# A chunked recurrence woven into projections: the order of its narrow matmuls and of three short VectorE and ScalarE steps

## The chip, the cores and the metric

The kernel runs on one core of one Trainium2 chip. The metric is the device time of one execution in microseconds. Before the change it is 2709.11 us, the median of 3 runs (2707.46 to 2709.36). A difference is read in per cent of that.

The engines are PE (TensorE: matmuls; PEld is its weight load), DVE (VectorE), ACT (ScalarE), POOL (GpSimd) and SP, which issues the DMAs. Each of them runs its own instructions in the order in which they were built, and they wait for one another by semaphores.

## The reference

One encoder layer over 2048 tokens of width 1024. A combined input projection `h @ w_in` feeds two branches: a bidirectional gated linear recurrence (HGRN2) of 8 heads of width 128, and neighbourhood attention of 16 heads of width 64. Both are gated, concatenated, projected out and normalised. The change is in the recurrence. Cut to that:

```python
b = jnp.cumsum(log_f, axis=3)
scores = jnp.einsum('bhntd,bhnsd->bhnts', q * jnp.exp(b - b_mid), k * jnp.exp(b_mid - b))
scores = jnp.where(lower_tri, scores, 0.0)
o_intra = jnp.einsum('bhnts,bhnsv->bhntv', scores, v)
def step(state, xs):
    qc, kc, vc, dc = xs
    o = jnp.einsum('bhtd,bhdv->bhtv', qc, state)
    state = dc[..., None] * state + jnp.einsum('bhtd,bhtv->bhdv', kc, vc)
    return state, o
...
o = direction(zf_fw, lb_fw, False) + direction(zf_bw, lb_bw, True)
o = _rmsnorm(o.transpose(0, 2, 1, 3), norm_g).reshape(B, S, HG_WIDTH)
return o.astype(g_in.dtype) * jax.nn.silu(g_in)
```

The two directions are computed with chunked scores inside a chunk and a state that passes between chunks. The output of each head is divided by the root of the mean of its squares and gated.

## The kernel before

The work is in float32. Large products are split in a high and a low part (`wh`, `wl`, `h`) and use three matmuls of 512 columns per 128 rows of weights. The program has a start and a first attention half, then the recurrence (16 rounds: 8 heads of the first 1024 tokens, 8 of the second), then the second attention half and the output projection.

**The recurrence.** `hgrn` handles one head of one half: two groups g = 0, 1 of 512 tokens, four chunks of 128 each. For a group:

- `rates` and `ends` make the decay sums `c` (the scans, L422), the factors `ei`, `qi`, `de` and the decays `dec`.
- `turned` (L447 on PE, L449 on ACT) transposes, `updates` (L455) multiplies keys by values per chunk, `forward_states` (L466, L468, DVE) runs the forward state through the four chunks, reading the `updates` result in PSUM.
- `diagonal_factors` (L479 to L485) makes `kx` and `qx`, each with one buffer: differences (L479, DVE), two exponentials (L481, L482, ACT), products (L483, L485, DVE).
- `diagonal` (L494) makes the scores of 32 by 32 blocks with matmuls on a quarter of PE's columns, four of them side by side (`tile_position=(0, j * 32)`).
- `level_factors` (L507 to L515) and `level` (L522) do the same for distances of 32 and 64, with matmuls on half of PE's columns. The factors have four buffers `x`.
- `masked` copies the levels' scores to `pm` (L528, ACT), copies the diagonal's scores by mask to `pdb` (L532, DVE, three per group) and adds them to `pm` (L535, DVE, four per group).
- `outputs` multiplies the values by `pm` (L546) and the forward states by `qi` (L548).

`hgrn_tail` finishes a head while the next one is under way: the backward states (L614, L616) and their products (L620), and in the second half `rms_out`: squares (L320, ACT), split in `rh` (L322, DVE) and `rl` (L324, DVE), summed over the head by two matmuls with ones (L327, L328), then root, product and gate (L330 to L334) and the DMA to `yT`. In the second half it also corrects the first half's tokens (L643, L644) and norms them.

**The order of the work.** PE's order is written by hand (`manual_schedule`). `weave` alternates the recurrence, which yields a number of units (54 per head), with `hgrn_dense`, the projections of the next head (L255, evacuated by ACT at L352 to L369, with L314 to L316 and L372 for the gate). A unit is about 1.5 steps of 3 matmuls, and the dense generator runs until its share is reached. So the number behind a `yield` sets how many projection matmuls stand at that place. `next(tail)` takes one step of the last head's tail. The order on DVE and ACT is set when the program is built: a scheduler takes what it holds for ready, the lowest place in the source first; `tc.high_priority(offset=PRI)` moves an instruction up by 1500 places. Weights come by DMA and are split by L245 (ACT) and L246 (DVE).

In before, the heart of a group reads:

```python
pb = diagonal(kx, qx)
lf = [(w, *level_factors(w, g, cs, ks)) for w in (32, 64)]
yield 6
next(tail, None)
pa = ps("pa")
for w, xk, xq in lf:
    level(w, pa, xk, xq)
pm = masked(pa, pb)
yield 5
outputs(g, v, pm)
```

Of the kernel before, what the change touches and what calls it, by code (L numbers as in the profile page):

```python
# [11 lines left out]
F32R = mybir.dt.float32r  # L12
U32 = mybir.dt.uint32
AF = mybir.ActivationFunctionType
ALU = mybir.AluOpType
# [4 lines left out]
P = 128  # L20
# [10 lines left out]
PRI = 1500  # L31
# [6 lines left out]
def body(ctx: ExitStack, tc: tile.TileContext, t):  # L38
    nc = tc.nc
    dve, act, pool, pe = nc.vector, nc.scalar, nc.gpsimd, nc.tensor  # L40
# [46 lines left out]
    def nm(s):  # L87
        cnt[0] += 1
        return f"{s}_{cnt[0]}"

    def tl(tag, dt=F32, shape=None):
        if tag in cur["smap"]:
            tag = cur["smap"][tag]
            return sh.tile([P, 512], dt, tag=tag, name=nm(tag), bufs=SH[tag])
        return cur["pool"].tile([P, 512] if shape is None else shape, dt, tag=tag, name=nm(tag), bufs=cur["bufs"].get(tag, 1))
# [4 lines left out]
    def ps(tag="mx"):  # L100
        if tag == "pj":
            return pp.tile([P, 512], F32, tag=tag, name=nm("pj"))
        tag = cur["map"].get(tag, tag)
        return cur["psum"].tile([P, 512], F32, tag=tag, name=nm("ps"), bufs=cur["ps"][tag])
# [211 lines left out]
        act.activation(e, e, AF.Exp, scale=-1.0)  # L316

    def rms_out(u, g, o_sb, sg, tok):
        sq = tl("t")
        act.activation(sq, o_sb, AF.Square)  # L320
        sh_ = tl("rh", F32R)
        dve.tensor_copy(sh_, sq)  # L322
        sl_ = tl("rl", F32R)
        dve.tensor_tensor(sl_, sq, sh_, op=ALU.subtract)  # L324
        yield
        pss = ps("ss")
        pe.matmul(pss, ones, sh_, start=True, stop=False)  # L327
        pe.matmul(pss, ones, sl_, start=False, stop=True)  # L328
        r = tl("t")
        act.activation(r, pss, AF.Ln, scale=1.0 / 128.0, bias=eps_rms)  # L330
        act.activation(r, r, AF.Exp, scale=-0.5)
        dve.tensor_mul(r, r, o_sb)
        yv = tl("t")
        dve.tensor_tensor(yv, r, sg, op=ALU.mult)  # L334
        dma(yT[u][:, tok:tok + 512], yv)
# [60 lines left out]
    def hgrn(u, half, st, tail):  # L396

        zs, qs, sgs, vts = st["e"], st["q"], st["sg"], st["v"]
        S = {}
        if half == 1:  # L400
            S[0, 0] = sfb[u]
        ubs, decs, qibs, os_ = {}, {}, {}, {}
        decb_all = tl("decb", shape=[P, 8])

        def rates(d, g):
            col = d * 8 + u
            e = zs[d, g]
            dve.tensor_scalar_min(e, e, ECAP)
            L = tl("g")
            act.activation(L, e, AF.Ln, bias=1.0)  # L410
            c = tl("c")
            act.activation(c, e, AF.Ln, scale=lbt[:, col:col + 1], bias=1.0)
            r = tl("g")
            act.activation(r, L, AF.Exp, scale=-1.0, bias=l1m[:, col:col + 1])
            dve.tensor_tensor(e, e, r, op=ALU.mult)
            for b in range(4):
                lo, hi = b * P, (b + 1) * P
                if d == 0:
                    sl = slice(lo, hi)
                else:  # L420
                    sl = slice(hi - 1, lo - 1 if lo else None, -1)
                dve.tensor_tensor_scan(c[:, sl], c[:, sl], L[:, sl], 0.0, op0=ALU.add, op1=ALU.subtract)  # L422
            return c, e

        def ends(d, g, c, k):
            last = 127 if d == 0 else 0
            ei = tl("ei")
            act.activation(ei, c, AF.Exp)
            dec = tl("dec", shape=[P, 4])
            dve.tensor_copy(dec, v4(ei, P)[:, :, last])  # L430
            decs[d, g] = dec
            if d == 1:
                dve.tensor_copy(decb_all[:, g * 4:g * 4 + 4], v4(ei, P)[:, :, last])
            qi = tl(f"qi{d}")
            dve.tensor_mul(qi, qs[g], ei)
            qibs[d, g] = qi
            de = tl("de")
            for b in range(4):
                sl = slice(b * P, (b + 1) * P)
                act.activation(de[:, sl], c[:, sl], AF.Exp, scale=-1.0, bias=c[:, b * P + last:b * P + last + 1])  # L440
            dve.tensor_mul(de, k, de)  # L441
            return de

        def turned(src, tag):
            pk = ps("tr")
            for b in range(4):
                pe.transpose(pk[:, b * P:(b + 1) * P], src[:, b * P:(b + 1) * P], ident)  # L447
            ke = tl(tag)
            act.activation(ke, pk, AF.Copy)  # L449
            return ke  # L450
# [7 lines left out]
        def forward_states(g, pu):  # L458
            for b in range(4):
                bb = g * 4 + b  # L460
                if half == 0 and bb == 7:
                    sn = sfb[u]
                else:
                    sn = tl("Sf", shape=[P, P])
                if (0, bb) in S:
                    dve.scalar_tensor_tensor(sn, S[0, bb], decs[0, g][:, b:b + 1], pu[:, b * P:(b + 1) * P], op0=ALU.mult, op1=ALU.add)  # L466
                else:
                    dve.tensor_copy(sn, pu[:, b * P:(b + 1) * P])  # L468
                S[0, bb + 1] = sn

        def diagonal_factors(g, cs, ks):
# [16 lines left out]
        def diagonal(kx, qx):  # L488
            pb = ps("pb")
            for b in range(4):  # L490
                for k0, n, dst in ((0, 64, b * 64), (32, 32, 256 + b * 32)):
                    for j in range(4):
                        o = (b * 4 + j) * 64
                        pe.matmul(pb[j * 32:(j + 1) * 32, dst:dst + n], kx[:, o + k0:o + k0 + 32], qx[:, o:o + n],  # L494
                                  start=True, stop=True, skip_group_check=True, tile_position=(0, j * 32))
            return pb

        def level_factors(w, g, cs, ks):
            n2 = 512 // (2 * w)
            xq, xk = tl("x"), tl("x")  # L500
            cv = {d: cs[d].rearrange("p (n s c) -> p n s c", s=2, c=w) for d in range(2)}
            kv = {d: ks[d].rearrange("p (n s c) -> p n s c", s=2, c=w) for d in range(2)}
            xqv = xq.rearrange("p (n s c) -> p n s c", s=2, c=w)
            xkv = xk.rearrange("p (n s c) -> p n s c", s=2, c=w)
            rf = cv[0][:, :, 0, w - 1:w].to_broadcast([P, n2, w])
            rb = cv[1][:, :, 1, 0:1].to_broadcast([P, n2, w])
            dve.tensor_tensor(xkv[:, :, 0, :], rf, cv[0][:, :, 0, :], op=ALU.subtract)  # L507
            dve.tensor_tensor(xqv[:, :, 1, :], cv[0][:, :, 1, :], rf, op=ALU.subtract)
            dve.tensor_tensor(xkv[:, :, 1, :], rb, cv[1][:, :, 1, :], op=ALU.subtract)
            dve.tensor_tensor(xqv[:, :, 0, :], cv[1][:, :, 0, :], rb, op=ALU.subtract)  # L510
            act.activation(xk, xk, AF.Exp)
            act.activation(xq, xq, AF.Exp)
            dve.tensor_mul(xkv[:, :, 0, :], xkv[:, :, 0, :], kv[0][:, :, 0, :])
            dve.tensor_mul(xkv[:, :, 1, :], xkv[:, :, 1, :], kv[1][:, :, 1, :])
            dve.tensor_mul(xq, xq, qs[g])  # L515
            return xk, xq
# [34 lines left out]
        for g in range(2):  # L551
            v = turned(vts[g], "v")
            next(tail, None)
            cs, ks = {}, {}
            cs[0], ks[0] = rates(0, g)
            yield 5
            next(tail, None)
            cs[1], ks[1] = rates(1, g)
            de0 = ends(0, g, cs[0], ks[0])
            yield 5  # L560
            next(tail, None)
            ke0 = turned(de0, "ke")
            de1 = ends(1, g, cs[1], ks[1])
            kx, qx = diagonal_factors(g, cs, ks)
            yield 3
            next(tail, None)
            forward_states(g, updates(ke0, v))
            ke1 = turned(de1, "ke")
            yield 3
            next(tail, None)  # L570
            pu = updates(ke1, v)
            if g == 0:
                ub = tl("ub")
                act.activation(ub, pu, AF.Copy)
                ubs[g] = ub
            else:
                ubs[g] = pu
            pb = diagonal(kx, qx)
            lf = [(w, *level_factors(w, g, cs, ks)) for w in (32, 64)]
            yield 6  # L580
            next(tail, None)
            pa = ps("pa")
            for w, xk, xq in lf:
                level(w, pa, xk, xq)
            pm = masked(pa, pb)
            yield 5
            outputs(g, v, pm)
        for _ in tail:
            pass
# [667 lines left out]
    with psum_phase("h", *HPS), phase("h", HB, SMH), tc.manual_schedule(engines={mybir.EngineType.PE}):  # L1257
        hgrn_init()
        tail = iter(())
        for i in range(16):  # L1260
            half, u = divmod(i, 8)
            if i < 15:
                nxt = hgrn_dense((i + 1) % 8, (i + 1) // 8, i in (6, 7), reload if i == 6 else None)
                tail, st = weave(hgrn(u, half, st, tail), nxt, HTOT, HSUM)
# [235 lines left out]
```

## Time and profile before

| what | value |
|---|---|
| median of 3 runs | 2709.11 us (2707.46 to 2709.36) |
| the profiled execution's own time | 2713.41 us |
| its span | 2711.6 us |
| PE busy | 2613.3 us, 96% of the span |
| DVE busy | 1763.9 us, 65% |
| ACT busy | 1420.5 us, 52% |
| DMA, mean | 109 GB/s |

The span is the time from the first to the last instruction of the profiled execution. A row of the timeline reads: start in us, duration in us, engine, line, operation, names of what is written and read, shape, count, and in brackets the idle time of the engine before it with what ended it. Rows of matmuls give a modelled end, so distances between starts are used for them; a float32 matmul of 128 or 64 columns shows as two records.

### The profile page before, as it was taken

How to read it: one execution, taken by the hardware profiler on the slowest of the kernel's cores; microseconds unless marked ns; L12 is line 12 of the kernel's file. 1: busy time of each engine (PE TensorE's matmuls, PEld its weight loads, DVE VectorE, ACT ScalarE, POOL GpSimd, SP SyncE). 2: the span in 40 equal slices, each digit the busy share in tenths (PEclk: the TensorE clock that was granted, in tenths of full speed). 3: DMA queues.
4: the chain of work that ended last, by engine and by line, in shares of the span. 5: the costliest groups of instructions: out<-in, count | busy, mean ns of one | idle time of the engine just before them, and what ended most of it. 6: DMA issues, size and time to landing. Idle time of an engine off the chain costs nothing.

```text
span 2711.6 us, 46035 instructions
## 1 busy us (share of the span) xinstructions
PE 2613.3 (96%) x17328; PEld 2157.5 (80%) x17328; DVE 1763.9 (65%) x4351; ACT 1420.5 (52%) x2808; POOL 104.9 (4%) x142
## 2 busy tenths in 40 slices
PE   4999999989999999999999999989999999899998
PEld 3788888878888888888888888877777777678887
DVE  5435445467777778877777877455777777648443
ACT  4434344366666666666666666444666666431110
POOL 0000000000000000000000000000000000032221
PEclk9999999999999999999999999999999999999999
DMA  7564454312111126212221222354444444444331
GB/s 248 159 183 139 130 172 139 117 52 75 63 57 61 63 74 218 82 41 75 75 79 59 67 67 86 107 159 119 125 129 126 127 131 138 110 136 140 97 93 55
DMA packets 226845, 296.46 MB, mean 109 GB/s; under 512 B 28743, under 2 KB 117575, under 8 KB 226503
## 3 DMA queue, kind: packets, MB, share of 16 engines
q1 hardware_dynamic: 226623, 293.52, 35.5%
q8 instruction: 136, 2.23, 0.4%
q14 instruction: 86, 0.70, 0.1%
HBM read 218.24 MB, written 66.99 MB: 105 GB/s over the span
## 4 chain that ended last, share of the span: by engine, by line
PE 71%; DVE 3%; DMA 3%; ACT 2%; issue 1%; SPq 0%; DVEq 0%; ACTq 0%
PE pj L255 38%; PE ps L1333 4%; PE ps L1332 4%; PE ps L1331 4%; PE ps L1041 3%; PE ps L1022 3%; PE pj L268 2%; PE ps L455 2%; PE ps L978 1%; PE ps L447 1%; PE ps L981 1%; PE ps L522 1%; PE ps L546 1%; PE ps L494 1%; PE ps L548 1%; DMA bias<-tint 1%
## 5 line engine op out<-in xcount | busy, mean ns | idle before, releaser
L255 PE MATMUL pj<-h,wh 128*128 128x512 f32 x4016 | 1289.2, 402 | 6.5 <-ACT wh L781 2.1
L255 PEld LDWEIGHTS pj<-h,wh 128*128 128x128 f32 x4016 | 728.3, 189 | 168.1 <-issue 21.5
L255 PE MATMUL pj<-h,wl 128*128 128x512 f32 x2008 | 789.1, 393 | 0.1
L255 PEld LDWEIGHTS pj<-h,wl 128*128 128x128 f32 x2008 | 378.6, 189 | 83.7 <-DVE wl L756 0.5
L995 ACT ACTIVATE pbuf<-pbuf,mx 128x480 f32<-128x480 f32 (+2 forms) x256 | 164.3, 643 | 177.5 <-DVE mx L990 176.8
L990 DVE CUSTOM_DVE_ANT_1 pbuf<-ps,bias 128x480 f32<-128x480 f32 (+2 forms) x256 | 144.0, 596 | 139.3 <-PE ps L981 124.7
L268 PE MATMUL pj<-wh,h 128*128 128x256 f32 x1024 | 197.0, 289 | 4.5 <-ACT vt L274 4.2
L268 PEld LDWEIGHTS pj<-wh,h 128*128 128x128 f32 x1024 | 164.5, 194 | 8.5 <-ACT vt L274 5.0
L245 ACT ACTIVATE wh<-wr 128x512 fp32r<-128x512 f32 x192 | 120.1, 626 | 82.4 <-PE pj L255 69.6
L246 DVE TENSOR_TENSOR wl<-wr,wh 128x512 fp32r<-128x512 f32 x192 | 131.7, 686 | 46.8 <-ACT wh L245 46.0
L268 PE MATMUL pj<-wl,h 128*128 128x256 f32 x512 | 146.0, 285 | 0.0
L1028 ACT ACTIVATE pt<-ps 128x512 f32<-128x512 f32 (+1 forms) x128 | 69.0, 539 | 124.6 <-PE ps L1022 124.3
L1026 DVE COPY pt<-ps 128x512 f32<-128x512 f32 (+1 forms) x128 | 79.4, 620 | 78.8 <-PE ps L1022 77.9
L1041 PE MATMUL ps<-pt,V 128*64 128x128 f32 x1408 | 108.3, 285 | 14.9 <-DVE pt L1026 6.0
L441 DVE TENSOR_TENSOR de<-e,de 128x512 f32<-128x512 f32 x64 | 44.3, 692 | 118.3 <-ACT de L440 117.2
L1022 PE MATMUL ps<-ident,pbuf 128*128 128x128 f32 x896 | 119.1, 273 | 0.8 <-DVE pbuf L1000 0.8
L1022 PEld LDWEIGHTS ps<-ident,pbuf 128*128 128x128 f32 x896 | 105.6, 141 | 17.1 <-issue 1.9
L1000 DVE TENSOR_SCALAR pbuf<-pbuf,mx 128x480 f32<-128x480 f32 (+2 forms) x256 | 108.0, 437 | 4.9
L1041 PEld LDWEIGHTS ps<-pt,V 128*64 128x64 f32 x1408 | 75.8, 137 | 43.5 <-issue 19.6
L1307 ACT ACTIVATE yh<-yr 128x512 fp32r<-128x512 f32 x52 | 32.7, 629 | 131.2 <-PE ps L1332 112.8
L268 PEld LDWEIGHTS pj<-wl,h 128*128 128x128 f32 x512 | 99.5, 194 | 0.7 <-issue 0.5
L1380 DVE TENSOR_TENSOR vt<-ps,gt 128x512 f32<-128x512 f32 x24 | 16.5, 692 | 127.2 <-PE ps L1333 127.2
(266 smaller groups left out, 4622.9 us busy)
## 6 DMA issues: line engine op xcount, KB each, us to landing
wr<-in_w_in SPq DMA_DIRECT2D x276, 256.0 KB
V<-nv SPq DMA_DIRECT2D x256, 64.0 KB
yr<-yq SPq DMA_DIRECT2D x64, 256.0 KB
bias<-tint SPq DMA_DIRECT2D x24, 480.0 KB
wr<-in_w_v SPq DMA_DIRECT2D x32, 256.0 KB
x<-in_x SPq DMA_DIRECT2D x32, 256.0 KB
ada<-in_ada_w SPq DMA_DIRECT2D x16, 512.0 KB
nv<-vt SPq DMA_DIRECT2D x32, 256.0 KB
```

What stands on the lines that cost most here:

```text
L245: act.activation(hi, raw, AF.Copy)
L246: dve.tensor_tensor(lo, raw, hi, op=ALU.subtract)
L255: pe.matmul(pz, a, b, start=(k == 0 and n == 0), stop=(k == KT - 1 and n == 2))
L268: pe.matmul(pzs[tp][:, i * 256:(i + 1) * 256], a, b, start=(k == 0 and n == 0 and i == 0), stop=(k == KT - 1 and n == 2), skip_group_check ...
L990: return dve.tensor_tensor_reduce(s[:, 0:nk].rearrange("p (r c) -> p r c", c=32), sc[:, 0:nk].rearrange("p (r c) -> p r c", c=32), bt[:, 0 ...
L995: act.activation(s[:, 0:nk], s[:, 0:nk], AF.Exp, scale=-1.0, bias=mx[:, 0:1], accum_out=mx[:, 1:2])
L1000: dve.tensor_scalar(s[:, 0:nk], s[:, 0:nk], mx[:, 2:3], 1.0, op0=ALU.mult, op1=ALU.mult)
L1022: pe.transpose(ptp[:, c * P:(c + 1) * P], s[:, c * P:(c + 1) * P], ident)
L1041: pe.matmul(self.po[R][hs_, j * P:(j + 1) * P], self.st.V[c0 + c][:, j * P + hh * 64:j * P + hh * 64 + 64], pts[hh][:, c * P:(c + 1) * P], ...
L1331: pe.matmul(pz, yh[:, kk], wh, start=first, stop=False)
L1332: pe.matmul(pz, yh[:, kk], wl, start=False, stop=False)
L1333: pe.matmul(pz, yl[:, kk], wh, start=False, stop=last)
```

## The change

There are three edits, all in the recurrence. The squares and their two parts in `rms_out` are put under `high_priority`. The forward states are put under `high_priority`. And in `hgrn` the call of `diagonal` moves behind the `yield` and the tail's step, directly in front of the levels; the level factors are then traced before it, and the two yields become 5 and 6 where they were 6 and 5.

```diff
     def rms_out(u, g, o_sb, sg, tok):
-        sq = tl("t")
-        act.activation(sq, o_sb, AF.Square)
-        sh_ = tl("rh", F32R)
-        dve.tensor_copy(sh_, sq)
-        sl_ = tl("rl", F32R)
-        dve.tensor_tensor(sl_, sq, sh_, op=ALU.subtract)
+        with tc.high_priority(offset=PRI):
+            sq = tl("t")
+            act.activation(sq, o_sb, AF.Square)
+            sh_ = tl("rh", F32R)
+            dve.tensor_copy(sh_, sq)
+            sl_ = tl("rl", F32R)
+            dve.tensor_tensor(sl_, sq, sh_, op=ALU.subtract)
         yield
...
-                if (0, bb) in S:
-                    dve.scalar_tensor_tensor(sn, S[0, bb], decs[0, g][:, b:b + 1], pu[:, b * P:(b + 1) * P], op0=ALU.mult, op1=ALU.add)
-                else:
-                    dve.tensor_copy(sn, pu[:, b * P:(b + 1) * P])
+                with tc.high_priority(offset=PRI):
+                    if (0, bb) in S:
+                        dve.scalar_tensor_tensor(sn, S[0, bb], decs[0, g][:, b:b + 1], pu[:, b * P:(b + 1) * P], op0=ALU.mult, op1=ALU.add)
+                    else:
+                        dve.tensor_copy(sn, pu[:, b * P:(b + 1) * P])
...
-            pb = diagonal(kx, qx)
             lf = [(w, *level_factors(w, g, cs, ks)) for w in (32, 64)]
-            yield 6
+            yield 5
             next(tail, None)
+            pb = diagonal(kx, qx)
             pa = ps("pa")
             for w, xk, xq in lf:
                 level(w, pa, xk, xq)
             pm = masked(pa, pb)
-            yield 5
+            yield 6
             outputs(g, v, pm)
```

More of the change, by code (lines that the diff above doesn't have):

```diff
@@ L577, in hgrn @@
                 ubs[g] = pu
+            lf = [(w, *level_factors(w, g, cs, ks)) for w in (32, 64)]
+            yield 5
+            next(tail, None)
             pb = diagonal(kx, qx)
-            lf = [(w, *level_factors(w, g, cs, ks)) for w in (32, 64)]
-            yield 6
-            next(tail, None)
             pa = ps("pa")
```

## The prediction

> **What bounds the kernel now.** I read the page's totals first, then the busy time of four stretches, then the list of who waited for whom on PE.
>
> ```profile
> span 2711.6 us, 46035 instructions
> PE 2613.3 (96%) x17328; PEld 2157.5 (80%) x17328; DVE 1763.9 (65%) x4351; ACT 1420.5 (52%) x2808; POOL 104.9 (4%) x142
> ...
> 602.00:900.00 298.00, 298.00 (x2236) 252.62 (x2236) 220.60 (x580) 185.39 (x342) 0.40 (x4) 1.00 0.19 62
> ...
> PE ps L455 <- DVE Sf L466: 8.2, 1, 8.2
> PE ps L327 <- DVE rh L322: 5.6, 9, 1.4
> PE ps L328 <- DVE rl L324: 1.8, 8, 0.2
> PE ps L546 <- DVE pm L535: 0.2, 1, 0.2
> ```
>
> The recurrence lies at about 600 to 1745 us, and there PE is busy all the time (298.00 of 298.00 us) at a granted clock of 1.00, while DVE is busy for 74% (220.60/298.00). Every PE instruction counts there, and so does every wait that PE gets. The change can remove little waiting: the waits on the norm squares (L327, L328) are 7.4 us, the one on the forward states (L455) 8.2 us, and the masked scores (L546) are waited for once, 0.2 us.
>
> **The diagonal moved in front of the levels.** The chain that ended last shows what the narrow matmuls cost around them (start, us, what).
>
> ```profile
> 698.81 0.89 PE ps L455 x8
> 699.71 0.83 PE ps L494 x64
> 700.54 6.33 PE pj L255 x27
> 706.87 1.08 PE ps L522 x32
> 707.95 5.00 PE pj L255 x21
> ...
> 715.17 5.47 PE pj L255 x24
> ```
>
> After the transposes, 24 projection matmuls take 5.47 us, 0.228 each. By that price the 27 after the diagonal (L494) would take 6.15, and take 0.18 more; the 21 after the levels (L522) would take 4.79, and take 0.21 more. So leaving narrow tiles costs some 0.2 us. After the change L494 stands directly before L522, and one of the two exits per group goes, but the step from 32 columns to 64 is in no row. Its bounds are the nearest rows: free (0.18 saved), or as dear as an exit (nothing saved). A loss I exclude within 0.02 us, since no exit is above 0.21. I take the middle, 0.10, for 32 groups (16 heads, two groups each): **-3.2 us**, bounds -5.8 to +0.6.
>
> The Trainium skill, "TensorEngine Tiling (Array Packing)", Key Properties, states that a change of tiling mode, not merely of the tile, drains TensorE. By that rule 32 to 64 columns is a switch too and may cost as much as an exit; the saving would be 0 and my sum 3.2 us higher. The rows agree that leaving a narrow mode costs time, and no row shows this switch.
>
> **What the move does to DVE.** The built order of the two kernels (line numbers of before throughout) shows it; for the groups g = 1:
>
> ```
> before: 532 479 616 479 532 532 616 483 485 485 314 | 507..510 507..510 | 535x4 372
> after:  616 616 314 532 479 479 532 532 | 507..510 507..510 | 372 535x4 483 485 485
> ```
>
> In before, the diagonal's three masked copies (L532) and the next group's differences (L479) ran in the 6.3 us between diagonal and levels. Now they can only begin when the diagonal ends, which is when the levels begin, and they stand ahead of L535, which finishes pm, for which PE waits at L546.
>
> ```profile
> 666.28 0.31 DVE L532 COPY_PREDICATED pdb<-mskd,ps 128x128 f32<-128x128 uint32 x1 [0.71 <-PE ps L494]
> 666.49 1.29 DVE L479 TENSOR_TENSOR kx<-c 128x512 f32<-128x512 f32 x2
> 667.69 0.49 DVE L532 COPY_PREDICATED pdb<-mskd,ps 128x128 f32<-128x128 uint32 x2
> ...
> 1276.59 1.15 PE L522 MATMUL ps<-x,x 128*64 128x64 f32 x32
> ...
> 1277.23 0.43 DVE L314 TENSOR_SCALAR gt<-gt 128x512 f32<-128x512 f32 x1 [1.23 <-ACT gt L369]
> 1277.57 0.42 DVE L507 TENSOR_TENSOR x<-c 128x256 f32<-128x256 f32 x1
> ...
> 1280.26 1.16 DVE L535 TENSOR_TENSOR pm<-pdb 32x128 f32<-32x128 f32 x4
> 1281.45 0.69 DVE L372 TENSOR_TENSOR sg<-gt,gt 128x512 f32<-128x512 f32 x1
> ...
> 1282.58 0.38 PE L546 MATMUL ps<-pm,v 128*128 128x128 f32 x2
> ```
>
> Count from the start of the levels. In before pm was ready at 4.83 (1281.42) and wanted at 5.99. In after it is wanted at 5.99 + 3 x 0.228 = 6.67, because 24 projection matmuls stand there in place of 21. DVE first does L314, which waits for the gate projection's exit on ScalarE; that projection's end lies 24 matmuls behind L455 in both kernels, directly before the diagonal now, so I leave L314 near where it was (0.55; row: 0.64). Then: L314 0.34, copies and differences 1.90 (666.28 to 668.18), eight differences 2.69 (1277.57 to 1280.26), L372 0.61 (its 0.69 less the 0.08 by which these rows overlap), L535 1.16. The end is 0.55 + 6.70 = 7.25, and PE starts some 0.05 later. **PE waits 0.6 us** per group (bounds 0.3 to 1.0). The order is the same in heads 0 to 5 and 8 to 14 (counted 0 to 15 over both halves): 13 x 0.6 = **+7.8 us**. The last head's g = 0, with 18 matmuls in that gap in both kernels, loses about **+1.3 us**: wanted at 1.08 + 5.00 - 3 x 0.228, or nearer 5.5, ready at about 7.0 by the sum below, less the 0.2 us that it waits already.
>
> Groups g = 0 are not caught by this: with 27 matmuls there, pm is wanted 0.68 later, at 7.4. In heads 9 to 14 DVE must first do L644 and L408 (first L532 at about 0.3), then 1.90 + 0.34 (L322) + 2.69 + 0.60 (L324) + 1.16 = 7.0. The cover left is 0.4 us; if it is gone, each of the 15 groups pays what is missing.
>
> **Norm squares and forward states "ahead".** In the built order every L466 and L468 keeps its neighbours, so the forward states gain nothing and the 8.2 us stay: I count 0. The norm squares move in heads 9 to 14, and the wrong way where it counts. First the step after the three products of L620:
>
> ```profile
> 1290.27 0.83 PE L620 MATMUL ps<-qi,Sb 128*128 128x128 f32 x6
> ...
> 1290.47 0.60 ACT L352 ACTIVATE e<-pj 128x512 f32<-128x512 f32 x1 [0.59 <-PE pj L255]
> 1291.13 0.60 ACT L622 ACTIVATE t<-ps 128x512 f32<-128x512 f32 x1
> ...
> 1292.30 0.62 ACT L428 ACTIVATE ei<-c 128x512 f32<-128x512 f32 x1
> 1292.82 0.62 ACT L410 ACTIVATE g<-e 128x512 f32<-128x512 f32 x1
> 1293.35 0.70 ACT L412 ACTIVATE c<-e,lbt 128x512 f32<-128x512 f32 x1
> ...
> 1293.07 0.69 DVE L324 TENSOR_TENSOR rl<-t,rh 128x512 fp32r<-128x512 f32 x1
> 1294.08 1.37 DVE L422 TENSOR_TENSOR_SCAN c<-c,g 128x128 f32<-128x128 f32 x4 [0.32 <-ACT c L412]
> ...
> 1295.75 0.40 PE L327 MATMUL ps<-rh,ones 128*128 128x512 f32 x1
> ```
>
> After's ScalarE order is 352, 428, 622, 315, 410, 412, 320; DVE's is the four scans L422, then 322, 372, 324. From the start of L620: L352 at 0.20, then five steps of 0.50 to 0.55 bring L412 to 2.8, its end to 3.5; scans 1.28, L322 0.34, L372 0.61, L324 0.69: rl is ready at 6.45, where before it was at 3.49. PE wants it at 5.7 (0.23 behind L327's 5.48). **PE waits 0.8 us** x 6 = **+4.8 us** (bounds 0 to 1.2 each).
>
> Second, the norm of the first half's tokens after L643, in the same heads:
>
> ```profile
> 1311.79 1.22 DVE L483 TENSOR_TENSOR qx<-qx,q 128x1024 f32<-128x1024 f32 x1
> ...
> 1319.47 1.16 DVE L535 TENSOR_TENSOR pm<-pdb 32x128 f32<-32x128 f32 x4
> ...
> 1322.40 0.38 PE L546 MATMUL ps<-pm,v 128*128 128x128 f32 x2
> ...
> 1332.04 0.69 DVE L644 TENSOR_TENSOR cl<-ps,cl 128x512 f32<-128x512 f32 x1
> 1333.43 0.43 DVE L322 CAST rh<-t 128x512 fp32r<-128x512 f32 x1 [0.70 <-ACT t L320]
> ...
> 1335.52 0.40 PE L327 MATMUL ps<-rh,ones 128*128 128x512 f32 x1
> 1335.75 0.40 PE L328 MATMUL ps<-rl,ones 128*128 128x512 f32 x1
> ...
> 1305.63 0.49 PE L327 MATMUL ps<-rh,ones 128*128 128x512 f32 x1 [0.37 <-DVE rh L322]
> 1306.36 0.50 PE L328 MATMUL ps<-rl,ones 128*128 128x512 f32 x1 [0.23 <-DVE rl L324]
> ```
>
> Count from L546. Before, L535 ended 1.77 us ahead of it and L644 ended at 10.33: 12.1 us of queue. After, L535 ends about 0.4 ahead, and the queue behind it gains L483 (1.22) and two L485 (of the shape of L479's pair, 1.2; all stood ahead of L535) and loses L324 (0.6) and the pauses in it. Those I take as 0.8 (with none of them gone it is 13.9, with the whole growth covered 12.1): 12.1 + 2.4 - 0.6 - 0.8 = 13.1 us. L644 ends at 12.7, L320 and L322 add 1.13, rh is ready at 13.8. PE wants it at 13.12: **0.7 us**. Where L327 waits for rh, L328 waits for rl too: 0.73 apart at 1305.63 against 0.23 at 1335.52, **0.5 us** more. 6 x 1.2 = **+7.2 us** (bounds 0 to 1.9 each). The waits that stand there already (1305.63) keep their order and follow L328 by the same chain; I count 0 for them. No DMA is added, and the SP queue moves by a few places of weight loads, which I cost at nothing: the weight halves L246 are needed a projection (16 steps) after they are made.
>
> **Sum.** -3.2 + 7.8 + 1.3 + 4.8 + 7.2 = +17.9. Against the profiled execution (2713.41 us, span 2711.6) that is 2731.3; it lies 4.3 above the median of the three runs, 2709.1, so I forecast **2727.0 us**.
>
> **The rivals.**
> - Heavier: the cover of 0.4 us in the g = 0 groups is gone as well (15 heads x 0.6 = 9 more) or each wait is at its upper bound: 2736 to 2746. For it speaks that DVE is busy for 74% on average and does these chains without a pause; against it that it still waits for others at 666.28 (0.71) and 1277.23 (1.23). Chance 0.15.
> - Only the wait for pm comes and the norm steps find their slack: -3.2 + 9.1 = +5.9, 2715. For it: the rows of L327 at 1295.75 and 1335.52 had 2.0 us (rl, 1293.76) and 1.7 us (rh, 1333.86) of slack. Chance 0.13; half of it counted as same.
> - Faster: the narrow matmuls follow each other free of cost (-5.8) and DVE has done L314, L532 and L479 in time, so that pm is not late: 2703. It decides on whether pm is ready within 6.67 us of the levels' start; the chain above would have to be 0.6 us shorter in 13 groups. Chance 0.06.
> - The change does nothing that counts: the switch inside the narrow pair costs what the exit did, and the waits stay within 0.2 us each: 2709 to 2713. Chance 0.06.
>
> The forecast has 0.60. Two tenths of a per cent (5.4 us) is about what a measurement of this kernel can tell from no change. Slower: 0.60 + 0.15 + 0.07 = 0.82; within 0.2%: 0.06 + 0.06 = 0.12; faster 0.06. The range takes in the pm-only case at its lower end and half of the heavier: 2711 to 2740.
>
> **What would show it.** The waits of PE: L546 on L535 some 9 us in 14 times, L328 on L324 and L327 on L322 up by some 12 together. In the chain, 455, 24 x 255, 494, 522: if the time from L494's start to the projection after the levels is 1.91 (0.83 + 1.08), the narrow pair joins as I took it or better; over 2.0, nothing is saved. If L546 does not wait in g = 1 groups, the DVE sum is wrong, and with it the sign.

## The result, and the profile after

The changed kernel takes 2728.22 us (median of 4 runs, 2727.28 to 2729.84) where the kernel before, on the same chip, takes 2709.24 (4 runs, 2707.46 to 2710.42): a ratio of 1.0068, 95% interval 1.0056 to 1.008. It is slower, by 19.0 us (0.7%); the forecast was 2727.0, within 2711 to 2740.

The totals of the changed kernel's page, then its busy times in two stretches of the recurrence (columns: stretch, its length, then busy us of PE, PEld, DVE, ACT, POOL, granted clock, DMA share, GB/s). Its lines are numbered one higher than before's from `rms_out` on and two higher from `forward_states` on.

```profile
span 2725.5 us, 45997 instructions
PE 2613.0 (96%) x17328; PEld 2153.0 (79%) x17328; DVE 1757.1 (64%) x4351; ACT 1417.0 (52%) x2808; POOL 104.7 (4%) x142
```

```profile
1200.00:1500.00 300.00, 289.67 (x2035) 236.46 (x2034) 230.26 (x538) 196.18 (x363) 0.00 (x0) 1.00 0.20 67
602.00:900.00 298.00, 296.40 (x2203) 250.65 (x2202) 219.11 (x574) 182.95 (x341) 0.40 (x4) 1.00 0.18 61
```

The first of these stretches in the kernel before:

```profile
1200.00:1500.00 300.00, 297.14 (x2175) 246.25 (x2174) 236.12 (x550) 199.57 (x371) 0.00 (x0) 1.00 0.22 71
```

The busy time of PE is the same as before (2613.0 against 2613.3) at the same granted clock of 1.00 in both stretches: no work was added, and the clock is no lower. PE stands idle. In the first half's heads that is 1.6 us of 298 (before: none), in the second half's 10.3 us of 300 (before: 2.9). The list of who waited says for what:

```profile
PE ps L328 <- DVE rh L323: 8.3, 14, 1.4
PE ps L456 <- DVE Sf L468: 8.1, 1, 8.1
PE ps L548 <- DVE pm L537: 6.9, 14, 1.7
PE ps L329 <- DVE rl L325: 6.9, 19, 0.7
```

Beside before's rows, the wait for pm is new (6.9 us in 14 against 0.2 in 1), the one for rl grew from 1.8 to 6.9 and the one for rh from 5.6 to 8.3; the wait for the forward states stays (8.1 against 8.2). The list counts the idle time between a modelled end and the next start; what a wait costs is read below from starts, and is more. The chain of the work that ended last shows both sides of the change in one picture (start, us, what):

```profile
662.44 0.89 PE ps L456 x8
663.33 5.49 PE pj L255 x24
668.82 0.84 PE ps L496 x64
669.66 1.08 PE ps L524 x32
670.74 6.35 PE pj L255 x27
...
697.50 5.51 PE pj L255 x24
703.03 0.69 ACT gt L368
703.72 0.49 ACT gt L370
704.24 0.43 DVE gt L314
704.88 1.19 DVE kx L481 x2
706.07 0.41 DVE pdb L534 x2
...
709.15 0.60 DVE sg L373
709.95 0.28 DVE pm L537
...
710.98 0.46 PE ps L548 x2
```

In the group g = 0 (at 663) diagonal and levels stand side by side and the chain never leaves PE. In g = 1 it leaves PE with the gate projection, goes through ScalarE's exit and a queue of DVE work, and comes back at L548: that is the new wait.

Three sums of starts in the trace give the sizes. One group g = 0 of a first-half head before: 0.987 (updates to diagonal) + 0.835 (to the projection) + 6.330 (27 matmuls) + 1.082 (levels) + 5.582 (24) = 14.816 us; after: 0.813 + 5.666 (24) + 0.835 + 1.082 + 6.260 (27) = 14.656. So the seam saves **0.16 us** a group. From the end of the levels to the outputs, 24 matmuls take 5.582 us undisturbed and 6.135 in after's g = 1: **0.555** in 13 groups, 7.2 us. And set side by side at the start of each head's outputs, after minus before runs from -2.5 us at head 0 to -1.2 at head 8 (counted 0 to 15), then climbs 2.5 us a head through heads 9 to 14 to +14.1, and is +14.2 at the last outputs: 16.7 us come in the recurrence. The spans differ by 13.9. The -2.5 is none of the change's: up to the recurrence PE has the same instructions in the same order in both kernels, and the two executions differ there in the granted clock. From 132.5 to 139 us, before and then after:

```profile
132.50:139.00 6.50, 5.29 (x15) 3.99 (x16) 0.98 (x5) 0.63 (x1) 0.00 (x0) 0.50 0.58 160
132.50:139.00 6.50, 5.95 (x32) 4.86 (x33) 3.25 (x8) 1.67 (x4) 0.04 (x1) 1.00 0.62 186
```

In that stretch after gains 4 us on before, 1.7 of it at a wait for a DMA (L1041: 3.2 us in before, 1.3 in after) and the rest while the clock differs; smaller differences leave 2.4 when L455 first starts. There all twelve other traces are ahead of this execution of before, by 1.7 to 4.0 us.

### The profile page after: what moved, and what is told of

Read it like the earlier page. It is cut to its first block, busy times and chain, and to the rows that moved or that the text cites. A ratio compares the mean times of both kernels' runs of the same rounds, so it can differ in the third digit from the quotient of the medians.

```text
span 2725.5 us, 45997 instructions
## 1 busy us (share of the span) xinstructions
PE 2613.0 (96%) x17328; PEld 2153.0 (79%) x17328; DVE 1757.1 (64%) x4351; ACT 1417.0 (52%) x2808; POOL 104.7 (4%) x142
## 4 chain that ended last, share of the span: by engine, by line
PE 61%; DVE 11%; ACT 3%; DMA 2%; issue 1%; SPq 0%; DVEq 0%; ACTq 0%
PE pj L255 31%; PE ps L1333 4%; PE ps L1335 4%; PE ps L1334 4%; PE ps L1043 3%; PE ps L1024 3%; PE pj L268 2%; PE ps L456 2%; PE ps L980 1%; PE ps L448 1%; PE ps L983 1%; PE ps L548 1%; DVE c L423 1%; DVE kx L481 1%; PE ps L550 1%
## 5 line engine op out<-in xcount | busy, mean ns | idle before, releaser
L268 PE MATMUL pj<-wh,h 128*128 128x256 f32 x1024 | 195.5, 288 | 5.4 <-ACT vt L274 5.1
L268 PEld LDWEIGHTS pj<-wh,h 128*128 128x128 f32 x1024 | 163.4, 193 | 9.3 <-ACT vt L274 5.8
L268 PE MATMUL pj<-wl,h 128*128 128x256 f32 x512 | 145.5, 284 | 0.0
L268 PEld LDWEIGHTS pj<-wl,h 128*128 128x128 f32 x512 | 98.9, 193 | 0.8 <-issue 0.5
```

Source lines behind the costliest of these rows:

```text
L268: pe.matmul(pzs[tp][:, i * 256:(i + 1) * 256], a, b, start=(k == 0 and n == 0 and i == 0), stop=(k == KT - 1 and n == 2), skip_group_check ...
```

## The experiments

Line numbers below are those of each kernel; only those with the priority blocks differ from before's. "The move alone" is the third edit without the other two.

**1. The two high-priority blocks alone** (the diagonal stays where it was).

```diff
-        sq = tl("t")
+        with tc.high_priority(offset=PRI):
+            sq = tl("t")
...
-                if (0, bb) in S:
+                with tc.high_priority(offset=PRI):
+                    if (0, bb) in S:
```

> Only the two priority edits; the diagonal stays where it was. My theory after the result: all of the change comes from the move of the diagonal, since with this kernel the built order on PE, DVE and ACT is the one of before, instruction for instruction. It expects 2709 us, within 2 of before, and PE waits on the norm squares of about 7 us as before. The rival, that the priority put the norm squares late (the prediction laid 12 us of norm waits beside that edit), expects some 2709 + 12 = 2721 us.

2711.07 us against 2711.36, ratio 0.9998 (0.9989 to 1.0007). The order of instructions on PE, DVE and ACT is before's, one for one, and so are the waits (5.3 us in 9 for rh, 1.8 in 8 for rl). The blocks change nothing.

**2. The move alone.**

```diff
-            pb = diagonal(kx, qx)
             lf = [(w, *level_factors(w, g, cs, ks)) for w in (32, 64)]
-            yield 6
+            yield 5
             next(tail, None)
+            pb = diagonal(kx, qx)
...
-            yield 5
+            yield 6
```

> The move of the diagonal alone, without the two high-priority blocks. Theory (the order of the instructions sets the time, and the move alone gives it): 2728, 1.0055 to 1.008 of the kernel before, with the same waits in the recurrence as the changed kernel's profile: 6.9 us in 14 for pm, 7.6 in 13 for rh, 6.9 in 19 for rl. Rival, the prediction's own reading (the priority blocks put the norm squares the wrong way): the two norm items, 4.9 and 7.6 us as measured, go and 2716 is left, 1.0025 of before, with the rh and rl waits back at 4.7 and 1.8.

2728.8 us, ratio 1.0067 (1.0053 to 1.008), with the changed kernel's waits:

```profile
PE ps L327 <- DVE rh L322: 8.2, 14, 1.4
PE ps L546 <- DVE pm L535: 7.0, 14, 1.7
PE ps L328 <- DVE rl L324: 7.0, 19, 0.7
```

The rival falls: the later norm squares come from the move too. Its built order is the changed kernel's on every engine.

**3. One step less cover for pm**: the move alone, with the yields left at 6 and 5, so that the pair stands a step of three matmuls later and the outputs where they were.

```diff
-            pb = diagonal(kx, qx)
             lf = [(w, *level_factors(w, g, cs, ks)) for w in (32, 64)]
             yield 6
             next(tail, None)
+            pb = diagonal(kx, qx)
```

> The move alone, with the yields left at 6 before the diagonal and 5 after the levels, so 3 projection matmuls (0.68 us) less stand between levels and outputs. Theory (PE waits for pm because the chain of copies, differences and adds is longer than that stretch): the wait at outputs in 13 groups g = 1 grows from 0.55 to about 1.24 us (+9), six groups g = 0 begin to wait by about 0.35 (+2): some 2739 us. Rival (the pair of narrow matmuls costs PE time by itself, wherever the outputs stand): no change against the changed kernel, 2728 us.

2727.82 us, 1.0059 (1.0045 to 1.0072): a miss for the theory of cover as it was put. In the groups g = 1 the wait for pm did not grow:

```profile
PE ps L546 <- DVE pm L535: 7.1, 14, 1.7
...
PE ps L327 <- DVE rh L322: 5.1, 8, 1.3
```

The timeline of DVE (start, us, engine, line, operation, out<-in, shape, idle before) tells why. First the changed kernel, then this one, in the same group:

```profile
1277.42 0.43 DVE L314 TENSOR_SCALAR gt<-gt 128x512 f32<-128x512 f32 x1 [4.74 <-ACT gt L370]
...
1282.85 1.17 DVE L537 TENSOR_TENSOR pm<-pdb 32x128 f32<-32x128 f32 x4
```

```profile
1277.41 0.43 DVE L314 TENSOR_SCALAR gt<-gt 128x512 f32<-128x512 f32 x1 [4.73 <-ACT gt L369]
...
1282.85 1.17 DVE L535 TENSOR_TENSOR pm<-pdb 32x128 f32<-32x128 f32 x4
```

In both DVE stands idle for 4.7 us at L314, which waits for the gate projection's exit, and from there the queue runs without a pause to pm, which ends 6.6 us later, at 1284.02 in both. The levels start 0.67 us later here (1277.62 against 1276.95) and it makes no difference. So pm is late because L314, and behind it the copies and differences that the move put there, stand ahead of it (before, DVE had done those and was idle for only 1.23 us at L314); in these groups, how many matmuls lie between levels and outputs matters only through where the outputs stand behind that gate projection. The other part of the theory came: in the six groups g = 0 of heads 9 to 14 the outputs start 0.20 us later (5.80 us against 5.60 from the end of the levels). That the total is the changed kernel's is in part a balance, since the norm step behind L643 waits 0.29 us before rh there instead of 0.78.

**4. Two steps more between gate and outputs**: the move alone with yields 4 and 7 (the lines of the move are left out here).

```diff
-            yield 6
+            yield 4
...
-            yield 5
+            yield 7
```

> The move alone, with yields 4 and 7: 6 projection matmuls (1.36 us) more stand between levels and outputs than in the changed kernel, with as many less in front of the diagonal. Theory: no wait for pm; the squares get back ahead of the logarithms in the built order, so the first norm wait (0.8 us x 6) goes, and the one after the correction falls from 1.27 to about 0.4 us x 6; the narrow pair still saves 0.16 us x 32 = 5.1: 2709 - 5.1 + 2 = about 2706 us. Rival (the pair costs by itself): 2728 us.

2726.08 us, 1.0052 (1.0039 to 1.0065), 20 above the forecast. The wait for pm is gone, but others are there:

```profile
PE ps L327 <- DVE rh L322: 6.4, 9, 2.2
PE pj L268 <- ACT gt L369: 5.6, 1, 5.6
```

By the starts of the outputs, head 9 loses 2.1 us, heads 10 to 14 lose some 0.7 each (after: 2.5 in each of these six), and the step to the last head alone loses 7.8, of which 5.6 is one wait for a gate's exit. Behind that wait the granted clock is 0.50 until 1676.4 us, and 15 matmuls of L268 start 0.21 us apart instead of 0.12, another 1.4 us:

```profile
1669.70:1676.30 6.60, 3.22 (x15) 3.22 (x16) 3.48 (x8) 3.04 (x5) 0.00 (x0) 0.50 0.25 82
```

A further loss is in no list of waits, since each piece is short (0.13 us of idle): in the 13 heads 0 to 5 and 8 to 14 the first projection matmul behind the six records of L620 starts 0.96 us after the first of these instead of 0.59, right behind the gate's exit on ScalarE (L369); that is 4.9 us. The cover cures the wait that it was made for, and waits for the gate's exit come in its place.

**5. All levels up to the diagonal**, the other way to make the pair: the diagonal keeps its place on PE, the levels and `masked` come right behind it, and the matmuls of both yields and the tail's step behind them. As in the changed kernel, the level factors are traced ahead of the diagonal.

```diff
-            pb = diagonal(kx, qx)
             lf = [(w, *level_factors(w, g, cs, ks)) for w in (32, 64)]
-            yield 6
-            next(tail, None)
+            pb = diagonal(kx, qx)
             pa = ps("pa")
             for w, xk, xq in lf:
                 level(w, pa, xk, xq)
             pm = masked(pa, pb)
+            yield 6
+            next(tail, None)
             yield 5
```

> The levels and the masked adds are moved up to the diagonal, directly behind L455, with yields 6 and 5 both behind them: the pair is as narrow as in the changed kernel, and pm has some 50 projection matmuls (11 us) of cover. Theory: no wait for pm, norm waits as in before (about 7 us, since the built order has the squares ahead of the logarithms again), the pair saves about 5 us: 2704 us. Rival (the pair costs by itself): 2728 us. If the change of columns from 32 to 64 cost what an exit costs: 2709 us.

2720.29 us, 1.003 (1.0021 to 1.0039), 16 above the forecast. In heads 0 to 6 the outputs come 0.20 us earlier with every group, from -3.76 to -6.45 us against before, and pm is never waited for. Head 9 then loses 2.8 us and each of heads 10 to 14 some 1.1, and that loss is where the norm step stands behind the outputs:

```profile
PE ps L327 <- DVE rh L322: 9.5, 15, 2.4
PE ps L328 <- DVE rl L324: 6.1, 14, 0.7
```

There L327 starts 0.93 us behind the start of the transposes instead of 0.36, and L328 1.20 behind L327 instead of 0.32. In head 9 the wait for rh behind 12 projection matmuls is 1.6 us longer besides. The last head loses 5.6 us: 2.2 are a wait for a gate's exit, and in two stretches of 3.4 us (from 1668.4 and from 1692.3 us) the granted clock is 0.50, where before's is 1.00. The seam is worth having; the place next to it is what has to be paid for.

**6. One step of three matmuls between diagonal and levels**, with the diagonal where the changed kernel has it and the yield behind the levels left at 5.

```diff
-            pb = diagonal(kx, qx)
             lf = [(w, *level_factors(w, g, cs, ks)) for w in (32, 64)]
-            yield 6
+            yield 5
             next(tail, None)
+            pb = diagonal(kx, qx)
+            yield 1
             pa = ps("pa")
```

> The move alone, but with one step of three projection matmuls between the diagonal and the levels, taken from the 18 ahead of the diagonal less one, so that 15 stand ahead, 3 between and 15 behind the levels beside the norm step's. Theory (what the pair saves is the second change of tile shape, 0.16 us a group): the change back and forth returns, 32 x 0.16 = 5.1 us, and the wait for pm grows by up to the three matmuls taken from its cover, 13 x 0 to 0.68: 2733 to 2742. Rival (the pair's place saves by itself and not by adjacency): no 5.1, 2728 to 2737, and the starts from the updates' last matmul to the levels' end are no longer than in the changed kernel but for the three matmuls.

2741.14 us, 1.0118 (1.0104 to 1.0133), within the theory's range. Its chain shows the seam:

```profile
669.95 0.84 PE ps L494 x64
670.78 0.88 PE pj L255 x3
671.66 1.08 PE ps L522 x32
```

Three projection matmuls take 0.88 us between two narrow groups, where three more in a long row cost 0.680 (the step from 48 to 51 matmuls in one stretch, 11.025 to 11.705 us, in the kernel of experiment 7): one way out and back costs **0.20 us**. The rival, that the place saves and not the adjacency, falls. The wait for pm grew by more than the three matmuls:

```profile
PE ps L546 <- DVE pm L535: 22.9, 22, 1.7
```

By the starts it is 1.49 us in 13 groups g = 1, 0.39 in two more (20.2 in all, against 7.2 in the changed kernel) and 0.68 in six groups g = 0; in g = 1 the product qx (L483, 1.2 us) now stands ahead of pm on DVE. The norm steps' new waits mostly fell away in exchange: by the starts 4.5 us less before rh and 6.2 less before rl. So the total lies in the range in part by a balance that was not forecast; what shows the seam is the 0.88.

**7. Levels up in half 0 of heads 0 to 6 alone**, where no norm step follows.

```diff
-            yield 6
-            next(tail, None)
+            up = half == 0 and u < 7
+            if not up:
+                yield 6
+                next(tail, None)
...
             pm = masked(pa, pb)
+            if up:
+                yield 6
+                next(tail, None)
             yield 5
```

> The other way round, and in half 0 of heads 0 to 6 alone (14 groups): the levels and the masked copies move up to stand right behind the diagonal, which stays where it was, and the 18 projection matmuls that stood between them come behind the levels, so that pm has 33 matmuls of cover. The rest of the kernel is as before. Theory (adjacency of diagonal and levels saves 0.16 to 0.21 us a group, and nothing is given back where the cover grows and no norm step follows): 14 x 0.20 = 2.8 us off, 2706.5, 0.999 of before, with no wait for pm. Rival (adjacency saves nothing by itself, what was measured in the changed kernel and in the kernel with all levels moved up was the shift of the projection matmuls): 2709.3, 1.000, stretches of heads 0 to 6 as long as before.

2710.57 us (11 runs) against 2710.95 (19 runs), 0.9998 (0.9989 to 1.0007). In its trace the outputs of these heads come 0.206 us earlier with each group, 2.7 us from the first to the fourteenth; 1.9 us of that is gone again by head 9: 0.7 at head 7, where L455 waits a second time, 0.4 us, for a forward state, and 1.2 at head 9, where L327 behind 12 projection matmuls starts 2.35 us behind the matmul before it instead of 1.17. In the last round this execution has a granted clock of 0.50 from 1683.5 to 1686.9 us, which takes 1.4 us more. The seam's 0.2 us is shown, the total of 2.8 is not: it is about as large as the interval.

**8. A third buffer for t, with the move**, and **9. with the levels up in half 0**, and **10. alone**. `t` holds a head's copied outputs (L622), their square from L320 to L324 and, in the same step, what the root and the product work on. It has two buffers.

```diff
-    HB = {"c": 3, "qi0": 1, "qi1": 2, "v": 2, "pm": 1, "ub": 1, "Sf": 5, "Sb": 5, "pd": 1, "dec": 4, "decb": 1, "dsuf": 1, "g": 3, "ei": 1, "de": 2, "ke": 1, "kx": 1, "qx": 1, "x": 4, "t": 2, "cl": 3, "rh": 1, "rl": 1}
+    HB = {"c": 3, "qi0": 1, "qi1": 2, "v": 2, "pm": 1, "ub": 1, "Sf": 5, "Sb": 5, "pd": 1, "dec": 4, "decb": 1, "dsuf": 1, "g": 3, "ei": 1, "de": 2, "ke": 1, "kx": 1, "qx": 1, "x": 4, "t": 3, "cl": 3, "rh": 1, "rl": 1}
```

> The move alone, and three buffers instead of two for the tile t that holds a square (and, one step later, the logarithm of the norm). Theory (the norm step behind the 12 projection matmuls waits because its square waits for a buffer of t, so that rh and rl stand behind two forward states on DVE; a third buffer takes them out): its wait of 0.56 before rh and 0.49 between rh and rl goes in 6 heads, 6.3 us, and 2728 becomes 2722, 1.0045 of before; the waits behind the fix product (1.27 a head) and behind the suffix product (0.82) stay, because other work stands ahead of them. Rival 1 (the buffer holds nothing up, ScalarE's queue does): 2728. Rival 2 (the third buffer takes all the norm waits out): 2728 - 6.3 - 4.9 - 7.6 = 2709.

> The levels moved up in half 0 of heads 0 to 6 as in the kernel beside it, and the third buffer for t. Theory: 2.8 us for the seam of 14 groups and 6.7 us for the norm step behind 12 projection matmuls, which waits 3.8 us in all before rh and 2.9 between rh and rl in the kernel before as well: 2709.2 - 9.5 = 2699.7, 0.9965 of before. Rival (the buffer isn't what the square waits for): 2706.5.

> The kernel before with the third buffer of t and nothing else. Theory (the buffer takes out the waits for rh and rl behind 12 projection matmuls, 6.7 us, and some more in the last round, as in the kernel with both edits, whose recurrence was 13 us shorter than that of the one with the levels moved up alone): 2700, 0.996 of before. Rival (the two edits need each other: the wait goes only with the levels moved up): 2707 or more.

With the move 2718.63 us, 1.0032 (1.0022 to 1.0042), 10 less than the move without it; with the levels up 2697.42, 0.9953 (0.9939 to 0.9966); alone 2702.05, 0.9968 (0.9957 to 0.9979). The buffer is worth 8.1 us alone (interval 5.7 to 11.7), 10.2 with the move and 13.2 with the levels up (2710.57 to 2697.42). That is more than the 6.3 and 6.7 forecast for the steps behind 12 matmuls, though alone 6.7 lies within the interval; in the trace of the kernel with the buffer alone 7.3 us come in heads 9 to 14, near what was worked out, and 3.3 more in the last round. Why shows on ScalarE. Before, then with the third buffer alone, the same step:

```profile
1301.38 0.60 ACT L622 ACTIVATE t<-ps 128x512 f32<-128x512 f32 x1 [1.10 <-DVE t L334]
1302.59 0.60 ACT L449 ACTIVATE ke<-ps 128x512 f32<-128x512 f32 x1 [0.61 <-PE ps L447]
...
1304.48 0.63 ACT L320 ACTIVATE t<-t 128x512 f32<-128x512 f32 x1
```

```profile
1296.16 0.60 ACT L622 ACTIVATE t<-ps 128x512 f32<-128x512 f32 x1 [0.92 <-PE ps L620]
1296.79 0.63 ACT L320 ACTIVATE t<-t 128x512 f32<-128x512 f32 x1
```

With two buffers L622 waits until L334 has read the last one, and the square is put behind five other steps (L449 and four L440); with three it follows at once, rh then stands ahead of the last two forward states on DVE and rl ahead of the last, and in the recurrence of the kernel with the buffer alone the waits for rh and rl are 1.0 us in one place, where before's were 4.7 and 1.8. In the move's kernel the waits that the move made are untouched:

```profile
PE ps L546 <- DVE pm L535: 7.1, 14, 1.7
PE ps L328 <- DVE rl L324: 5.4, 12, 0.7
```

so what the buffer saves and what the move costs are two things. The version with both edits of experiment 9 is the fastest of the study: 13.5 us faster than the kernel before. By the starts of the outputs up to head 14 its recurrence is 2.7 us shorter than that with the buffer alone, which is the seam of 14 groups.

**11. The third buffer and the levels up in both halves**, in half 1 with the tail's step and the matmuls of both yields behind them (in the groups g = 0 of heads 9 to 14 that is 15 matmuls, not the 9 expected, then the L643 product and 36 matmuls).

```diff
+            up = half == 0 and u < 7 or half == 1 and u < 7
+            a = 6 if half == 0 else 3
...
-            yield 5
+            if up:
+                yield a
+                next(tail, None)
+            yield 11 - a if up else 5
```

> The third buffer of t, and the levels moved up right behind the diagonal in both halves of heads 0 to 6, in half 1 with 9 projection matmuls and the norm step's call behind them and 24 matmuls more ahead of the outputs. Theory (each adjacent pair saves 0.2 us and what it gave back in the second-half heads with all levels moved up was the norm step behind the outputs, which now comes with more room): 2697.4 - 7 x 0.2 = 2696, 0.995 of before. Rival (the norm steps of heads 9 to 14 wait again, 1.4 us a head, as where all levels were moved up): 2697.4 + 7 x 1.2 = 2706.

2706.95 us, 0.999 (0.9981 to 0.9999): the rival. L327 and L328 wait again in six places, at the norm step behind the outputs, 1.5 us each time, as with all levels up:

```profile
PE ps L328 <- DVE rl L324: 4.2, 6, 0.7
PE ps L327 <- DVE rh L322: 3.0, 7, 0.8
```

## Why the prediction was right

**The sign and the total** were right: 2727.0 forecast, 2728.2 measured. Its sum was +17.9; in the recurrence of the two traces there are 16.7. Part of the nearness is luck: the terms' errors cancel, and the forecast set the sum against the median through an execution that lay 4.3 above it, while after's lay 0.9 below its own. Some 2.5 us of what before's execution is late stand ahead of the recurrence.

**The seam** (-3.2): right in kind, too small. It is 0.16 us in 25 groups and not 0.10, and some 0.19 in the seven where the L643 product stands in the stretch: -5.4 for 32. Where the pair stands directly behind L455 (experiments 5 and 7) it is 0.21 a group. From L496's start to L524's it is 0.835 us, as from the diagonal to a projection matmul in before, and the sign that the prediction named, 1.91 us from the diagonal to the projection behind the levels, came out at 1.917. By the Trainium skill, "TensorEngine Tiling (Array Packing)", Key Properties, a change of tiling mode drains TensorE, and by it the sum would have been 3.2 us higher. The runs don't show the step from 32 to 64 columns to be as dear as that, nor to be free: the first level matmul starts 0.126 us behind the last diagonal one, while the starts inside the diagonal are at most 0.06 apart. They show the cost where narrow tiles and whole ones meet: 0.20 us for a way out and back (experiment 6).

**The wait for pm** (+7.8): right, 0.555 us in 13 groups, 7.2. The working had L314 at 0.55 us behind the levels' start and pm ready at 7.25; the trace has 0.47 and 7.07. PE starts 0.14 us behind that and not 0.05, which brings the wait back to the forecast. The working took L314's wait for the gate as a start that the move leaves alone, and experiment 3 shows that this is what fixes pm's time. The groups g = 0 of heads 0 to 14 do not wait: their 27 matmuls take 6.26 us in all of them. With that, and with each wait below its upper bound, the heavier rival falls.

**The last head's g = 0** (+1.3): 1.57 (6.130 against 4.562 us for the 18 matmuls).

**The norm step behind L620** (+4.8): 0.82 us x 6 = 4.9, by the path that was worked out:

```profile
1295.53 1.37 DVE L423 TENSOR_TENSOR_SCAN c<-c,g 128x128 f32<-128x128 f32 x4 [0.62 <-ACT c L413]
...
1297.13 0.69 DVE L373 TENSOR_TENSOR sg<-gt,gt 128x512 f32<-128x512 f32 x1
1297.73 0.68 DVE L325 TENSOR_TENSOR rl<-t,rh 128x512 fp32r<-128x512 f32 x1
...
1298.47 0.50 PE L329 MATMUL ps<-rl,ones 128*128 128x512 f32 x1 [0.67 <-DVE rl L325]
```

The scans and the gate's difference L373 stand ahead of rl, which ends at 1298.41; PE starts on it at once.

**The norm step behind L643** (+7.2): 0.78 before rh and 0.49 before rl, 1.27 x 6 = 7.6.

```profile
1336.73 0.69 DVE L646 TENSOR_TENSOR cl<-ps,cl 128x512 f32<-128x512 f32 x1
1338.12 0.43 DVE L323 CAST rh<-t 128x512 fp32r<-128x512 f32 x1 [0.62 <-ACT t L321]
...
1338.60 0.51 PE L328 MATMUL ps<-rh,ones 128*128 128x512 f32 x1 [0.63 <-DVE rh L323]
1339.33 0.50 PE L329 MATMUL ps<-rl,ones 128*128 128x512 f32 x1 [0.22 <-DVE rl L325]
```

L646 (L644 in before) comes late, and the square, rh and rl follow it one by one. The two norm steps make 12.5 us by the starts, against 12.0 forecast; the list of waits, which the prediction named as the sign (up by some 12), shows 7.8 more for rh and rl. Missed here: in the last round one such wait that stood in before is gone (-1.0).

**The forward states** (0): right, their 8.2 us wait stays at 8.1.

**Where the reasoning failed.** "Norm squares and forward states 'ahead'" put the norm squares' new places under the priority blocks' heading, as if these had moved them. Experiments 1 and 2 show that the blocks move nothing, and that all of the reordering comes from the diagonal's place: moving one group of matmuls changes what is ready on DVE and ScalarE for every step behind it. The terms were right because they were read from the built order; what they were put down to was not.

A term was missing as well. The terms above add to some 15 us of the 16.7. What comes behind a wait is slower too: the sixteen records of the outputs take 1.86 us instead of 1.78 in the 13 groups (1.0 us in all), and the transposes start 0.34 us behind L329 instead of 0.24 in the 12 norm steps (1.2). The norm step behind 12 projection matmuls waits 0.5 less in all than in before. With these the sum is within 0.2 us of what the traces show. What stays open is why the granted clock falls to 0.50 at other places in one execution than in the next.

## What to carry to other kernels

Put matmuls of a narrow tile beside each other only where what they release is not the last link of another engine's queue: here 0.16 to 0.21 us a group were won on TensorE and up to 2.5 us a head were paid in waits for VectorE. To find what a result waits for, look at the first idle time of its engine ahead of it (4.74 us at L314), not at the work next to it. And before an order is changed by hand or by priority, compare the built orders of one edit at a time: here one edit of three did everything, and one buffer more was worth 8 us without moving a matmul.

## What the runs showed of the hardware

- Matmuls on 64 columns behind matmuls on 32 start as soon as whole projection matmuls do there (0.835 us from the first diagonal matmul, 0.126 from the last one, in both cases). Three whole matmuls between two narrow groups cost 0.198 us more than the same three in a row of their kind.
- A first part that comes late makes the second late as well: where L327 waited for rh behind 12 matmuls or behind L643, L328 started 0.73 us behind it instead of 0.23, since rl ends 0.7 us after rh on VectorE.
- What starts behind a short wait of PE takes a little longer: outputs that waited 0.4 us for pm take 1.86 us instead of 1.78, and transposes that follow an L329 that waited start 0.34 us behind it instead of 0.24.
- Behind a wait of 5.6 us (experiment 4) the granted clock was 0.50 until 1676.4 us, and the matmuls of L268 started 0.21 us apart instead of 0.12.
